# Gate matrix grouped by four expert tiles in DRAM, and a wider spacing of the score tiles

## The chip, the core and the metric

The kernel runs on one core of one Trainium2 chip. Times are device microseconds (us) of the program, from its start to its end. The engines are TensorE (PE; its weight loads are shown apart as PEld), VectorE (DVE), ScalarE (ACT), GpSimd (POOL) and SyncE (SP). SP and ACT issue ordinary DMAs (the queues q1 and q10 of the profile), POOL issues the indirect ones (q0), and all of them run on the same sixteen DMA engines.

## The reference, cut to what matters

A layer has a token mixer and then an expert layer (PEER) over 1024 tokens of width 1024. The change touches the expert layer alone. Each token has 8 heads; each head picks 16 of 16384 experts (128 x 128 product keys), with a softmax over the 16 as gates. Expert e adds gate x gelu(u_e . token) x v_e.

```python
def peer(h, wq, k1, k2, u, v):
    ...
    expert = (jnp.take_along_axis(i1, top_c // PEER_TOPK, axis=-1) * PEER_N_KEYS
              + jnp.take_along_axis(i2, top_c % PEER_TOPK, axis=-1))
    gate = jax.nn.softmax(top_s, axis=-1)
    ...
        act = jax.nn.gelu(jnp.einsum("pd,ped->pe", xb, jnp.take(u, eb, axis=0)), approximate=False)
        return jnp.einsum("pe,ped->pd", (gb * act).astype(v.dtype), jnp.take(v, eb, axis=0))
```

## The kernel before

The 1024 tokens are 8 blocks of 128. Five of them (`DB`: 2, 3, 5, 6, 7, so 640 tokens, `TD`) go the dense way, three (`GB`: 0, 1, 4) the gathered way.

**Dense.** The 16384 experts are 128 tiles of 128. For one tile, `u_load` and `u_turn` bring the rows of `u`, transpose them on PE (`put`, two PSUM buffers) and split them into two f16 halves (`uT`: high half on ACT, low half on POOL by way of `uf`). `u_act` makes the scores of 640 tokens with 48 matmuls (`ph0` and `ph1`, one PSUM buffer each) and applies the gelu on ACT into `ac`, a *score tile*. The scores of 80 of the 128 tiles (`early`, those with `e * 5 % 8 < 5`) are made ahead of time and kept in DRAM (`act_d`, 320 KB each); the other 48 (`live`: 1, 3, 6, 9, ...) are made when they are needed.

**Gates.** `route` finds a block's chosen experts and gates on DVE. `gate_block` builds the dense gate matrix of 32 tokens at a time: for each *chunk* of four tokens DVE writes one-hot rows (`oh`, two instructions), PE multiplies them (`pgm`, 8 matmuls into one PSUM buffer), and ACT copies the result into `gs` (two buffers of 2 MB). After eight chunks the ACT queue stores `gs` into `G_d`. There are 20 such stores and 160 chunks.

**Gathered.** For each of the 128 choices of a token, POOL gathers rows of `u` and of `v` by indirect DMAs (768 in all, 512 KB each, six buffers), and DVE takes a dot product (`row_False`, line 919) or adds into `gacc` (`row_True`, line 924).

**Stages around the change.** `prep` is a generator that runs the routes of blocks 0, 1 and 2, the gating of blocks 2 and 3, the key choice of the second half (`choosing(1)`), and the gating of 5, 6 and 7. It yields a planned cost after each step: 1.65 after a chunk, 16 after a route, 167.6 over the key choice. The loop at its end (lines 1115 to 1122) adds these costs up, and whenever `U_US` (6.2) have come together it places one early score tile (`early_tile`), and with it `G_E` (3.4) gathers once two blocks are routed. Then the expert stage begins, 32 groups of four expert tiles. For a group, the ACT queue loads its gates (`gt4`, two buffers); for each tile the scores are loaded (`acr`) or made, `v_tile` loads and splits the rows of `v`, and `weigh` multiplies scores by gates on DVE and splits them (`w16`: ACT cast, line 1140, and DVE, line 1141). While group g is weighed, `out_unit` multiplies group g - 1 on PE (`pe`, 24 matmuls for each of the five blocks) and DVE adds the result into `acc`. The remaining gathers are spread over the groups by `feed`.

The order of instructions on each engine is set when the program is built, by a scheduler that goes by this program order and the buffers; on the chip each engine runs its list in order. So a wait on ACT also holds the DMAs behind it in the ACT queue.

```python
G_d = dram.tile([TD // NB, P, P, NB], F32, name="G_d")
st_(out=G_d[DB.index(n) * (P // NB) + nb], in_=gs)
st_(out=gt4, in_=G_d[:, :, g * GR:(g + 1) * GR, :].rearrange("b i j n -> i b j n"))
```

In `G_d` a 32-token slice of one second key lies together for all first keys. So a store writes 16 KB for each of the 128 partitions, and a load for four expert tiles reads, for each partition, 20 pieces (one for each 32 tokens) of 4 x 32 x 4 = 512 bytes.

Of the kernel before, what the change touches and what calls it, by code (L numbers as in the profile page):

```python
# [55 lines left out]
R_C, R_CC, R_GM, R_GF, R_AB, R_LB, R_GKB, R_HN, R_GN = 0, 8, 16, 24, 32, 64, 96, 104, 105  # L56


U_US = 6.2
G_E = 3.4  # L60
CS = ((4, 4, 4, 4, 4, 4, 3, 3), (1, 1, 1, 1), 1, 0)
FILL = (0, 0, 2, 0, 0, 1, 1, 0)
# [5 lines left out]
def tile_layer(ctx: ExitStack, tc: tile.TileContext, x, c, ctxt, c_ctx, ada_w, ada_b, norm_mix_g,  # L68
# [51 lines left out]
    yg_d = dram.tile([KC, P, 2, T], F16, name="yg_d")  # L120
    m_d = dram.tile([2 * KC, P, T], F32, name="m_d")
    h2_d = dram.tile([len(GB), P, D], F32, name="h2_d")
    G_d = dram.tile([TD // NB, P, P, NB], F32, name="G_d")
    early = [e for e in range(NKEY) if e * 5 % 8 < 5]
    act_d = dram.tile([len(early), P, TD], F32, name="act_d")

# [823 lines left out]
    def u_load(e):  # L950
        un = pu.tile([P, D], F32, name=f"un{e}", tag="un", bufs=2)
        ld(out=un, in_=u_r[e])
        return un

    def u_turn(e, un):

        uT = pu.tile([P, 2, KC, P], F16, name=f"uT{e}", tag="uT", bufs=2)
        for q in range(2):
            pt = ppu.tile([P, 512], F32, name=f"put{e}_{q}", tag="put", bufs=2)
            for k in range(4):  # L960
                PE.transpose(pt[:, k * P:(k + 1) * P], un[:, (q * 4 + k) * P:(q * 4 + k + 1) * P], ident)  # L961
            pv = pt.rearrange("p (a b) -> p a b", a=4)
            hi, lo = uT[:, 0, q * 4:q * 4 + 4, :], uT[:, 1, q * 4:q * 4 + 4, :]
            S.activation(hi, pv, AF.Copy, scale=SU)  # L964
            uf = pu.tile([P, 4, P], F32, name=f"uf{e}_{q}", tag="uf", bufs=2)
            S.activation(uf, pv, AF.Copy, scale=SU)  # L966
            pace[0] = G.tensor_tensor(out=lo, in0=uf, in1=hi, op=ALU.subtract)  # L967
        return uT
# [15 lines left out]
    with ExitStack() as st:  # L984
# [68 lines left out]
        def gate_block(rT, n, nb):  # L1053

            gs = pg.tile([P, P, NB], F32, name=f"gs{n}_{nb}", tag="gs", bufs=2)
            for t0 in range(0, NB, TB):
                c0 = nb * NB + t0
                oh = pg.tile([P, 4, P, TB], F16, name=f"oh{n}_{c0}", tag="oh", bufs=4)
                cols_ = lambda j: rT[:, j:j + 2, c0:c0 + TB].unsqueeze(2).to_broadcast([P, 2, P, TB])
                tt(V, oh[:, 0:2], iota.unsqueeze(1).to_broadcast([P, 2, P, TB]), cols_(0), ALU.is_equal)  # L1060
                vmark[0] = V.tensor_tensor(out=oh[:, 2:4], in0=oh[:, 1:2].to_broadcast([P, 2, P, TB]), in1=cols_(2), op=ALU.mult)
                pgm = ppg.tile([P, TB, P], F32, name=f"pgm{n}_{c0}", tag="go")
                for t in range(TB):
                    for j in (2, 3):
                        PE.matmul(pgm[:, t, :], lhsT=oh[:, 0, :, t], rhs=oh[:, j, :, t], start=j == 2, stop=j == 3)  # L1065
                S.activation(gs[:, :, t0:t0 + TB].rearrange("p i n -> p n i"), pgm, AF.Copy, scale=SA / SG)  # L1066
                yield 1.65
            st_(out=G_d[DB.index(n) * (P // NB) + nb], in_=gs)

        def gating(blocks, sel):  # L1070
            for bi, n in enumerate(blocks):
# [27 lines left out]
        def early_tile():  # L1099
            nonlocal uT, pend  # L1100
            e = pend
            pend = next(es, None)
            uTn = u_turn(pend, u_load(pend)) if pend is not None else None
            ac = u_act(e, uT)
            st_(out=act_d[early.index(e)], in_=ac)
            uT = uTn
# [7 lines left out]
        for dt in prep():  # L1114
            t_ += dt
            while t_ >= U_US and pend is not None:
                t_ -= U_US
                early_tile()
                if len(gsel) > 1:
                    gathers(G_E)  # L1120
        while pend is not None:
            early_tile()
    prep_st.close()
    if "G" in dbg:
        ld(out=dbg["G"], in_=G_d)
# [9 lines left out]
    def weigh(e, ac, gt4):  # L1135

        v3 = ac.rearrange("p (b n) -> p b n", n=NB)
        tt(V, v3, v3, gt4[:, :, e % GR, :], ALU.mult)
        w16 = pd.tile([P, 2, TD], F16, name=f"w16_{e}", tag="w16", bufs=2 * GR)
        S.copy(w16[:, 0], ac)  # L1140
        vmark[0] = V.tensor_tensor(out=w16[:, 1], in0=ac, in1=w16[:, 0], op=ALU.subtract)
        return w16
# [21 lines left out]
    NU = len(DB)  # L1164
    NG = NKEY // GR
    live = [e for e in range(NKEY) if e not in early]
    uT = u_turn(live[0], u_load(live[0]))
    li = 0
    work = lambda e: 2.1 if e in early else 9.5
    left = [sum(map(work, range(NKEY))), 256 * len(GB) - done[0]]  # L1170

# [4 lines left out]
    for g in range(NG + 1):  # L1176
        cur = None
        if g < NG:
            gt4 = pd.tile([P, TD // NB, GR, NB], F32, name=f"gt{g}", tag="gt4", bufs=2)
            st_(out=gt4, in_=G_d[:, :, g * GR:(g + 1) * GR, :].rearrange("b i j n -> i b j n"))  # L1180
            cur = ([None] * GR, [None] * GR)
            for j in range(GR):
                e = g * GR + j
                if e in early:
                    ac = pu.tile([P, TD], F32, name=f"acr{e}", tag="ac", bufs=3)
                    ld(out=ac, in_=act_d[early.index(e)])
                else:
                    uTn = None
                    if li + 1 < len(live):
                        uTn = u_turn(live[li + 1], u_load(live[li + 1]))  # L1190
                    ac = u_act(e, uT)
                    uT = uTn
                    li += 1
                cur[1][j] = v_tile(e)
                feed(work(e) / 3)
                cur[0][j] = weigh(e, ac, gt4)
                feed(work(e) / 3)
                if prev is not None:
                    for n in DB[j * NU // GR:(j + 1) * NU // GR]:
                        out_unit(g - 1, n, *prev)  # L1200
                feed(work(e) / 3)
        else:
            for _ in gth:
                pass
            m5 = pd.tile([P, D], F32, name="m5", tag="gt4", bufs=2)
            fg = pd.tile([P, D], F32, name="fg", tag="gt4", bufs=2)
            ld(out=m5, in_=mod_d[1:2, :].partition_broadcast(P).rearrange("p a d -> p (a d)"))
            ld(out=fg, in_=final_g.partition_broadcast(P))
            x1s = {}
            for n in range(NT):  # L1210
                x1s[n] = pd.tile([P, D], F32, name=f"x1_{n}", tag="v16", bufs=2 * GR)
                ld(out=x1s[n], in_=x1_d[n * P:(n + 1) * P, :])
                if n in DB:
                    out_unit(g - 1, n, *prev)
                a = acc[n]
                tt(V, a, a, m5, ALU.mult)
                tt(V, a, a, x1s[n], ALU.add)
                ss = pu.tile([P, 2], F32, name=f"fss{n}", tag="fss", bufs=3)
                sq = pu.tile([P, D], F32, name=f"fsq{n}", tag="uT", bufs=2)
                S.activation(sq, a, AF.Square, accum_out=ss[:, 0:1])  # L1220
                S.activation(ss[:, 1:2], ss[:, 0:1], AF.Sqrt, scale=1.0 / D, bias=eps)
                V.reciprocal(out=ss[:, 1:2], in_=ss[:, 1:2])
                V.scalar_tensor_tensor(out=a, in0=a, scalar=ss[:, 1:2], in1=fg, op0=ALU.mult, op1=ALU.mult)
                st_(out=out[n * P:(n + 1) * P, :], in_=a)
        prev = cur
# [27 lines left out]
```

## Time and profile before

| what | us |
|---|---|
| median of 3 runs | 4217.43 (4216.97 to 4219.64) |
| the profiled execution | 4229.67 |
| its span, first to last instruction | 4228.0 |
| PE busy | 3884.8 (92%) |
| DVE busy | 2938.6 (70%) |
| POOL busy | 1683.9 (40%) |
| ACT busy | 1430.1 (34%) |
| DMA traffic | 884.64 MB, 209 GB/s over the span |

A busy share is a mean over stages with different limits: PE is the busiest engine almost everywhere, while DVE and the DMA engines are busy only in the second half, where the expert layer runs. So the stages are read one by one, from tables of stretches; the granted clock is that of PE as a share of full speed, and the DMA share is the mean of the sixteen engines.

### The profile page before, as it was taken

To read this page: it belongs to the slowest core of one execution; us is meant where nothing else is said; L and a number is where in the kernel's file an instruction comes from. 1 tells how busy PE (TensorE), PEld (TensorE's weight loads), DVE (VectorE), ACT (ScalarE), POOL (GpSimd) and SP (SyncE) were. 2 spreads that over 40 slices of the span, in tenths; PEclk is the share of its full clock that TensorE was granted. 3 is DMA by queue.
4 is the path that set the end of the run, shared out by engine and by line. 5 is a ranking of instruction groups with operands and counts; after the bars stand their busy time and mean duration, and the time that the engine had idled before them with its cause. 6 is when DMAs were issued, how large, how long until landed. Compare 5 with 4: busy or idle time off the path is not lost.

```text
span 4228.0 us, 60334 instructions
## 1 busy us (share of the span) xinstructions
PE 3884.8 (92%) x23802; PEld 2350.2 (56%) x23802; DVE 2938.6 (70%) x5132; ACT 1430.1 (34%) x2194; POOL 1683.9 (40%) x1197
## 2 busy tenths in 40 slices
PE   6999999999999999988999989986899989999997
PEld 2665665656655444445776667763445544444453
DVE  5345446242556414379987799977989999889998
ACT  5344444243343202034543334552222222222222
POOL 2011111010011012127655567635766666666663
PEclk9999999999999999999999999987999999999998
DMA  5222122221223583227887778869989999989996
GB/s 189 78 73 85 56 73 79 74 87 46 87 64 115 162 282 107 99 97 242 295 307 249 254 242 298 305 228 319 329 318 336 321 323 325 316 311 325 328 315 232
DMA packets 435306, 884.64 MB, mean 209 GB/s; under 512 B 28511, under 2 KB 245066, under 8 KB 431438
## 3 DMA queue, kind: packets, MB, share of 16 engines
q0 software_dynamic: 110592, 402.70, 27.3%
q1 hardware_dynamic: 202676, 320.19, 22.6%
q10 hardware_dynamic: 121754, 157.89, 10.6%
q8 instruction: 186, 3.05, 0.3%
q14 instruction: 98, 0.80, 0.1%
HBM read 764.80 MB, written 115.88 MB: 208 GB/s over the span
## 4 chain that ended last, share of the span: by engine, by line
PE 47%; DVE 25%; DMA 11%; issue 8%; ACT 6%; POOL 4%; SPq 0%; ACTq 0%; DVEq 0%; POOLq 0%
PE ph L100 5%; DVE row_False L919 5%; PE pe L100 5%; DVE gacc L924 4%; PE pgm L1065 3%; PE pq L100 3%; PE pj_f0h L100 3%; PE pv_g L100 2%; PE pv_h L100 2%; DMA row_False<-in_peer_u_dram,idx 2%; PE pj_f1h L100 2%; PE pj_m L100 2%; DMA vn<-in_peer_v_dram 2%; DMA acr<-act_d 2%; PE pso L100 2%
## 5 line engine op out<-in xcount | busy, mean ns | idle before, releaser
L100 PE MATMUL pe<-v,w 128*128 128x512 f16 x3840 | 883.8, 392 | 138.7 <-DVE acc L1162 104.7
L100 PE MATMUL ph<-hb,uT 128*128 128x256 f16 (+1 forms) x6144 | 892.2, 303 | 14.6 <-POOL uT L967 10.4
L100 PEld LDWEIGHTS <-uT 128*128 128x128 f16 x6144 | 609.4, 99 | 242.5 <-POOL uT L967 13.1
L100 PEld LDWEIGHTS <-w 128*128 128x128 f16 x3840 | 384.0, 100 | 623.0 <-issue 166.4
L940 POOL DMA_INDIRECT row_False<-in_peer_u_dram,idx x384 | 548.9, 1429 | 274.6 <-DVE row_False L919 169.2
L940 POOL DMA_INDIRECT row_True<-in_peer_v_dram,idx x384 | 503.6, 1311 | 264.1 <-DVE gacc L924 173.1
L924 DVE SCALAR_TENSOR_TENSOR gacc<-row_True,dots,gacc 128x1024 f32<-128x1024 f32 x381 | 539.7, 1416 | 39.4 <-DMA row_True<-in_peer_v_dram,idx 35.8
L919 DVE SCALAR_TENSOR_TENSOR row_False<-row_False,h2n 128x1024 f32<-128x1024 f32 x384 | 496.2, 1326 | 67.1 <-DMA row_False<-in_peer_u_dram,idx 66.7
L967 POOL TENSOR_TENSOR uT<-uf,uT 128x512 f16<-128x512 f32 x256 | 380.8, 1499 | 284.0 <-ACT uf L966 282.6
L93 ACT ACTIVATE v<-vn 128x1024 f16<-128x1024 f32 x128 | 135.1, 1055 | 501.9 <-DMA vn<-in_peer_v_dram 386.7
L979 ACT ACTIVATE ac<-ph 128x256 f32<-128x256 f32 (+1 forms) x256 | 110.1, 438 | 371.8 <-PE ph L100 367.1
L1065 PE MATMUL pgm<-oh 128*128 128x128 f16 x1280 | 176.4, 295 | 53.2 <-ACT gs L1066 38.8
L1066 ACT ACTIVATE gs<-pgm 128x512 f32<-128x512 f32 x160 | 171.0, 1069 | 136.6 <-PE pgm L1065 136.6
L94 DVE SCALAR_TENSOR_TENSOR v<-vn,v 128x1024 f16<-128x1024 f32 x128 | 168.2, 1314 | 50.5 <-ACT v L93 50.3
L1162 DVE TENSOR_TENSOR acc<-pe,acc 128x1024 f32<-128x1024 f32 x155 | 188.6, 1217 | 11.8 <-PE pe L100 11.7
L100 PE MATMUL pj_m<-hb,w_m 128*128 128x512 f16 x768 | 187.4, 401 | 2.3 <-DVE lf_g L86 1.6
L1065 PEld LDWEIGHTS <-oh 128*128 128x128 f16 x1280 | 145.7, 117 | 77.0 <-issue 63.5
L100 PE MATMUL pq<-hb,w_wq 128*128 128x512 f16 x768 | 180.0, 387 | 1.0 <-POOL hb L89 0.8
L964 ACT ACTIVATE uT<-put 128x512 f16<-128x512 f32 x256 | 155.0, 605 | 71.0 <-PE put L961 69.4
L89 DVE TENSOR_TENSOR oh<-iota,rTr 128x1024 f16<-128x1024 f16 x160 | 139.1, 879 | 33.9 <-PE pgm L1065 33.8
L100 PEld LDWEIGHTS <-hb 128*128 128x128 f16 x1536 | 150.2, 98 | 17.8 <-issue 0.3
L966 ACT ACTIVATE uf<-put 128x512 f32<-128x512 f32 x256 | 154.4, 603 | 8.9 <-POOL uT L967 8.8
(364 smaller groups left out, 5531.9 us busy)
## 6 DMA issues: line engine op xcount, KB each, us to landing
un<-in_peer_u_dram SPq DMA_DIRECT2D x128, 512.0 KB
vn<-in_peer_v_dram SPq DMA_DIRECT2D x128, 512.0 KB
G_d<-gs ACTq DMA_DIRECT2D x20, 2048.0 KB
gt<-G_d ACTq DMA_DIRECT2D x32, 1280.0 KB
act_d<-ac ACTq DMA_DIRECT2D x80, 320.0 KB
acr<-act_d SPq DMA_DIRECT2D x80, 320.0 KB
mw<-in_ada_w_dram SPq DMA_DIRECT2D x32, 512.0 KB
w_wq<-wq_d SPq DMA_DIRECT2D x32, 512.0 KB
```

Of the source, the lines that this page charges most:

```text
L89: eng.tensor_tensor(out=out, in0=in0, in1=in1, op=op)
L94: return V.scalar_tensor_tensor(out=lo, in0=src, scalar=float(scale), in1=hi, op0=ALU.mult, op1=ALU.subtract)
L100: PE.matmul(ps, lhsT=a(k), rhs=b(k), start=n == 0, stop=n == last)
L919: V.scalar_tensor_tensor(out=row, in0=row, scalar=1.0, in1=h2n, op0=ALU.mult, op1=ALU.mult, accum_out=dots[:, s:s + 1])
L924: V.scalar_tensor_tensor(out=gacc[n], in0=row, scalar=dots[:, s:s + 1], in1=gacc[n], op0=ALU.mult, op1=ALU.add)
L940: G.indirect_dma_start(out=row, out_offset=None, in_=src[0], in_offset=bass.IndirectOffsetOnAxis(ap=gsel[n][0][:, s:s + 1], axis=0))
L964: S.activation(hi, pv, AF.Copy, scale=SU)
L966: S.activation(uf, pv, AF.Copy, scale=SU)
L967: pace[0] = G.tensor_tensor(out=lo, in0=uf, in1=hi, op=ALU.subtract)
L1065: PE.matmul(pgm[:, t, :], lhsT=oh[:, 0, :, t], rhs=oh[:, j, :, t], start=j == 2, stop=j == 3)
L1066: S.activation(gs[:, :, t0:t0 + TB].rearrange("p i n -> p n i"), pgm, AF.Copy, scale=SA / SG)
L1162: vmark[0] = V.tensor_tensor(out=acc[n], in0=ps, in1=acc[n], op=ALU.add)
```

## The change

`G_d` is laid out by groups of four expert tiles: [group, second key, 32-token slice, tile in the group, token]. A load of one group's gates is then one contiguous 10 KB row for each partition; a store of one slice goes out in 32 pieces of 512 bytes for each partition, 4096 in all.

`U_US` goes from 6.2 to 7.2, so early score tiles and their gathers are spaced wider in `prep`. The loop that made the remaining early tiles at the end of `prep` is gone. What is left (`rest`) is put into the first group of the expert stage: a list `todo` orders the tiles that have to be made (two left ones behind each weighing of group 0, the live ones in between), and `next_act` always transposes the tile after the one whose scores it makes. The left tiles are stored into `act_d` like the others and loaded in the last groups.

```diff
-U_US = 6.2
+U_US = 7.2
...
-    G_d = dram.tile([TD // NB, P, P, NB], F32, name="G_d")
+    G_d = dram.tile([NKEY // GR, P, TD // NB, GR, NB], F32, name="G_d")
...
-            st_(out=G_d[DB.index(n) * (P // NB) + nb], in_=gs)
+            st_(out=G_d[:, :, DB.index(n) * (P // NB) + nb].rearrange("g k a n -> k g (a n)"),
+                in_=gs.rearrange("k (g a) n -> k g (a n)", a=GR))
...
-        while pend is not None:
-            early_tile()
...
-    uT = u_turn(live[0], u_load(live[0]))
-    li = 0
+
+    rest = [pend, *es] if pend is not None else []
+    todo = []
+    for j in range(GR):
+        todo += [j] * (j in live) + rest[2 * j:2 * j + 2]
+    todo += rest[2 * GR:] + [e for e in live if e >= GR]
+    if not rest:
+        uT = u_turn(todo[0], u_load(todo[0]))
+    ahead_ = iter(todo[1:])
+
+    def next_act(e):
+        nonlocal uT
+        en = next(ahead_, None)
+        uTn = u_turn(en, u_load(en)) if en is not None else None
+        ac = u_act(e, uT)
+        uT = uTn
+        return ac
+
...
-            st_(out=gt4, in_=G_d[:, :, g * GR:(g + 1) * GR, :].rearrange("b i j n -> i b j n"))
+            st_(out=gt4, in_=G_d[g])
...
-                    uTn = None
-                    if li + 1 < len(live):
-                        uTn = u_turn(live[li + 1], u_load(live[li + 1]))
-                    ac = u_act(e, uT)
-                    uT = uTn
-                    li += 1
+                    ac = next_act(e)
...
+                if g == 0:
+                    for r in rest[2 * j:2 * j + 2] if j < GR - 1 else rest[2 * j:]:
+                        st_(out=act_d[early.index(r)], in_=next_act(r))
```

On ACT, near the end of the gating of block 7 (third of its four stores; `gs` are the copies of the chunks, the other rows belong to tiles), there stands before:

```order
L1066 ACTIVATE gs7_2_24701<-pgm7_68_24718 128x4x128
L964 ACTIVATE uT9_25283<-put9_1_25293 128x512
L966 ACTIVATE uf9_1_25299<-put9_1_25293 128x512
L1066 ACTIVATE gs7_2_24701<-pgm7_72_24731 128x4x128
L1066 ACTIVATE gs7_2_24701<-pgm7_76_24744 128x4x128
L1066 ACTIVATE gs7_2_24701<-pgm7_80_24757 128x4x128
L1066 ACTIVATE gs7_2_24701<-pgm7_84_24770 128x4x128
```

and in the changed program, at the same chunks:

```order
L1066 ACTIVATE gs7_2_23951<-pgm7_68_24052 128x4x128
L966 ACTIVATE uf117_0_24123<-put117_0_24117 128x512
L964 ACTIVATE uT117_24116<-put117_1_24126 128x512
L1066 ACTIVATE gs7_2_23951<-pgm7_72_24065 128x4x128
L966 ACTIVATE uf117_1_24132<-put117_1_24126 128x512
L979 ACTIVATE ac116_24135<-ph0_116_24136 128x256
L1066 ACTIVATE gs7_2_23951<-pgm7_76_24078 128x4x128
L1066 ACTIVATE gs7_2_23951<-pgm7_80_24091 128x4x128
L1066 ACTIVATE gs7_2_23951<-pgm7_84_24104 128x4x128
L979 ACTIVATE ac116_24135<-ph1_116_24162 128x384
L1106 DMA act_d_81<-ac116_24135 128x640
```

Score tiles 116 and 117 now stand between chunks that stood alone; the last of the 75 tiles that are made here is 119.

On ACT at the hand-over (the last gate store, the first gate load `gt0`, the first weighing's cast `w16_0`) there stands before:

```order
L1066 ACTIVATE gs7_3_24807<-pgm7_124_24902 128x4x128
L1068 DMA G_d_80<-gs7_3_24807 128x4096
L1180 DMA gt0_24949<-G_d_80 128x20x128
L93 ACTIVATE v16_0_24955<-vn0_24953 128x1024
L93 ACTIVATE v16_1_25041<-vn1_25039 128x1024
L1180 DMA gt1_25193<-G_d_80 128x20x128
L1140 CAST w16_0_24959<-acr0_24951 128x640
```

and in the changed program:

```order
L1068 DMA G_d_80<-gs7_3_24228 128x32x128
L966 ACTIVATE uf122_1_24551<-put122_1_24545 128x512
L979 ACTIVATE ac120_24554<-ph0_120_24555 128x256
L979 ACTIVATE ac120_24554<-ph1_120_24581 128x384
L964 ACTIVATE uT1_24610<-put1_0_24611 128x512
L1209 DMA act_d_81<-ac120_24554 128x640
L1195 DMA gt0_24520<-G_d_80 128x2560
L93 ACTIVATE v16_0_24526<-vn0_24524 128x1024
L966 ACTIVATE uf1_0_24617<-put1_0_24611 128x512
L964 ACTIVATE uT1_24610<-put1_1_24620 128x512
L966 ACTIVATE uf1_1_24626<-put1_1_24620 128x512
L979 ACTIVATE ac122_24629<-ph0_122_24630 128x256
```

Behind these rows come the second half of the scores of tile 122 and then the first cast, `w16_0`. So the scores of tiles 120 and 122 and the transposes of tile 1 now stand between the last gate store and that cast; tiles 124, 125 and 127 follow behind it, before any output matmul of group 0.

## Rows read from the trace of the kernel before

**Rows 1.** The page's part 2: PE, granted clock and DMA in 40 slices of 105.7 us.

```profile
PE   6999999999999999988999989986899989999997
...
PEclk9999999999999999999999999987999999999998
...
DMA  5222122221223583227887778869989999989996
```

**Rows 2.** Windows: start:end, length, each engine's busy us (instructions), clock, DMA share, GB/s.

```profile
1890.00:1986.90 96.90, 79.11 (x554) 59.29 (x553) 96.54 (x186) 46.00 (x75) 62.50 (x41) 0.91 0.63 205
1986.90:2189.60 202.70, 192.89 (x1458) 152.97 (x1456) 179.02 (x246) 106.13 (x164) 128.11 (x96) 1.00 0.84 302
2189.60:2500.00 310.40, 301.72 (x2028) 204.38 (x2027) 251.25 (x973) 102.58 (x200) 178.49 (x153) 0.99 0.75 257
2500.00:2799.40 299.40, 272.30 (x2029) 215.10 (x2028) 283.26 (x319) 155.28 (x243) 207.24 (x144) 0.97 0.82 295
2799.40:2858.70 59.30, 40.17 (x297) 32.79 (x296) 31.17 (x42) 30.49 (x36) 5.87 (x5) 0.76 0.35 140
2858.70:2876.30 17.60, 0.00 (x0) 0.00 (x0) 1.22 (x1) 2.11 (x2) 0.00 (x0) 0.50 0.84 291
2876.30:2907.80 31.50, 15.99 (x77) 8.11 (x78) 27.57 (x39) 9.48 (x15) 22.26 (x15) 0.72 0.94 321
2907.80:4167.00 1259.20, 1159.08 (x6148) 614.33 (x6149) 1144.82 (x1250) 329.47 (x512) 819.37 (x569) 0.96 0.92 321
```

**Rows 3.** Timeline of the ACT queue in 2650 to 2700: start, length, queue, line, issue.

```profile
2656.80 0.33 ACTq L1068 DMA_DIRECT2D G_d<-gs  x1
...
2681.35 0.33 ACTq L1068 DMA_DIRECT2D G_d<-gs  x1
...
2692.39 0.33 ACTq L1105 DMA_DIRECT2D act_d<-ac  x1
...
2699.78 0.33 ACTq L1105 DMA_DIRECT2D act_d<-ac  x1
```

**Rows 4.** Timeline of 2833 to 2838, PE and ACT: start, length, instruction, idle before.

```profile
2834.08 1.11 PE L1065 MATMUL pgm<-oh 128*128 128x128 f16 x8 [1.14 <-ACT gs L1066]
...
2835.23 1.04 ACT L1066 ACTIVATE gs<-pgm 128x512 f32<-128x512 f32 x1 [1.20 <-PE pgm L1065]
...
2836.33 1.11 PE L1065 MATMUL pgm<-oh 128*128 128x128 f16 x8 [1.13 <-ACT gs L1066]
```

**Rows 5.** Timelines of 2857 to 2909: ACT queue, DVE, PE.

```profile
2858.65 0.33 ACTq L1068 DMA_DIRECT2D G_d<-gs  x1
...
2865.03 0.40 ACTq L1180 DMA_DIRECT2D gt<-G_d  x1
...
2876.32 0.83 DVE L89 TENSOR_TENSOR acr<-acr,gt 128x640 f32<-128x640 f32 x1 [4.62 <-DMA vn<-in_peer_v_dram]
...
2907.76 8.17 PE L100 MATMUL pe<-v,w 128*128 128x512 f16 x28 [1.44 <-DVE w L1141]
```

**Rows 6.** Groups by line, 2500 to 2799.4: busy us, mean ns, idle before.

```profile
L924 DVE SCALAR_TENSOR_TENSOR gacc<-row_True,dots,gacc 128x1024 f32<-128x1024 f32 x86 | 129.4, 1505 | 12.2 <-DMA row_True<-in_peer_v_dram,idx 11.8
```

**Rows 7.** DMA queues, 2859 to 2866: packets, MB, share of 16 engines.

```profile
q10 hardware_dynamic: 144, 2.10, 70.8%
```

**Rows 8.** DMA queues, 1620 to 1650.

```profile
q10 hardware_dynamic: 2176, 1.05, 11.8%
```

**Rows 9.** DMA queues, 2960 to 4100.

```profile
q0 software_dynamic: 62757, 228.51, 56.0%
q1 hardware_dynamic: 31798, 102.24, 24.5%
q10 hardware_dynamic: 72150, 36.71, 11.4%
```

**Rows 10.** Chain of waits, 2907 to 4167: shares by line.

```profile
by line: PE pe L100 14.1%; issue 14.1%; DVE row_False L919 13.0%; DVE gacc L924 10.3%; DMA vn<-in_peer_v_dram 6.5%; DMA acr<-act_d 6.3%; DVE acc L1162 4.8%; DMA row_False<-in_peer_u_dram,idx 4.6%; DVE v L94 4.4%; DVE acr L89 3.8%; DVE w L11
```

**Rows 11.** Groups by line, 2907.8 to 4167.

```profile
L924 DVE SCALAR_TENSOR_TENSOR gacc<-row_True,dots,gacc 128x1024 f32<-128x1024 f32 x242 | 333.4, 1378 | 4.3 <-DMA row_True<-in_peer_v_dram,idx 1.7
```

## The prediction

> **What bounds the kernel now.** I read the slices of the page first [rows 1]: TensorE (PE) is busy in nine tenths or more of nearly every slice, with one dent at about two thirds of the span, where its granted clock falls to 0.7 as well. The DMA engines climb from two or three tenths to nine at the same place. So the next view is a table of stretches, cut at events of the ACT queue [rows 2]. In order they are: the first routes (1890 to 1986.9 us), gating blocks 2 and 3 (A, to 2189.6), the key choice of the second half (B, to 2500), gating 5 to 7 while score tiles last (C, to 2799.4), gating without score tiles (tail, to 2858.7), the wait for the gates (to 2876.3), the first weighing (to 2907.8), and the expert stage (to 4167).
>
> Three things are to be seen. In A and B PE is busy 95% and 97%, so it bounds them; in C PE has 91% and VectorE (DVE) 95%, so both do. From 2799.4 to 2907.8 nothing bounds: PE is busy 56 of 108 us, with the granted clock at 0.5 to 0.76, and DVE is busy 60. In the expert stage PE has 92%, DVE 91% and the DMA engines 92%: three limits within a point.
>
> Why the dent is there: a score tile costs PE 7.4 us where nothing else runs (from one score store to the next), and a block of eight chunks and its tiles lasts some 25 us from gate store to gate store [rows 3]. A gating chunk costs PE 1.1 us, but alone it takes 2.25 us, because PE waits for ACT to empty the one `pgm` buffer and ACT waits for PE [rows 4]. The tail is such chunks one after another, and then comes a chain of DMAs: the last gate block is stored at 2858.65, the first gate load starts 6.4 us later, and the first weighing starts at 2876.32, so 17.7 us in all, with PE idle and the clock at 0.5 (1.2 GHz). The first long run of output matmuls starts at 2907.76 [rows 5].
>
> **The spacing (6.2 to 7.2).** The planner's costs in `prep` sum to 543.6: 160 chunks at 1.65, seven routes at 16, and 167.6 for the key choice. At 6.2 the 80 tiles end after 496, and some 28 chunks are left bare, which is the tail. At 7.2 there is room for 75 tiles, to the last chunk; 5 are left. With each tile go 3.4 gathers, so 5 x 3.4 = 17 gathers move behind the hand-over as well. Stage by stage, with tiles at 7.4 us:
>
> A holds some 2.4 tiles fewer, or 18 us of PE. DVE loses 2.4 x 3.4 gathers at about 1.4 us, and would have 167 of 186 us. I take 16. B holds 167.6/6.2 - 167.6/7.2 = 3.75 tiles fewer, 28 us, with DVE at 81%; I take 26. The first routes give nothing, as DVE is full there (96.5 of 96.9). C with its tail: 206.4 of the costs lie there, so 28.7 tiles instead of 26.1, all between chunks. PE needs 28.7 x 7.4 + 96 x 1.1 = 318 us, and at its 91% of C that is 349. DVE had 283 + 31 and gets 2.6 x 3.4 = 9 more gathers at 1.5 [rows 6], so 328, or 345 at its 95%. Against 358.7 now I take 11 less. Sum: the last gate store comes 53 us sooner.
>
> **The written pieces.** Each of the 20 gate stores goes from 128 pieces of 16 KB to 4096 of 512 bytes. Now one takes 70.8% of 7 us, 4.96 us of the sixteen engines, or 423 GB/s [rows 7]. The nearest row for 512-byte writes is the store of the expert input `h_d`: 11.8% of 30 us for 1.05 MB, 297 GB/s, or 27.7 ns a piece [rows 8]. A store would take 7.1 us then, 2.1 more, 42 us of DMA time in A and C. There the engines have 16 to 18% free, and two `gs` buffers give each store a whole block to land. So I put 4 us on the path; 0 and 42 are the bounds. The last gate store is then at 2858.7 - 53 + 4 = 2809.7.
>
> **The read pieces.** Each of the 32 gate loads goes from 2560 pieces of 512 bytes to 128 of 10 KB. The ACT queue in the expert stage is nearly all gate loads: 11.4% of 1140 us for 36.71 MB, 282 GB/s; beside it the SP queue has 366 and the gathers 358 [rows 9]. At 366 a load takes 3.6 us instead of 4.65, so 34 us less in all; at the 423 of the 16 KB pieces, 50. No row shows a 10 KB piece, and 0 is the lower bound. Against it stand 17 gathers of 0.524 MB at 358 GB/s, 25 us. Net 9 us of 1160 busy. The chain of waits through the expert stage has 17% on three kinds of load (`vn`, `acr`, `row_False`) [rows 10], about 220 us; they shorten by 1 to 2%, so I take 4 us off, and keep 0 and 25. The Trainium skill ("DMA: Bandwidth & Descriptors", Specifications) puts the least transfer for line rate at 512 bytes. By that rule neither side of the new layout costs or gains anything, and the sum below would be 37 again (4 lost, 4 gained, both gone); the rows at 282 and 297 beside 423 GB/s do not bear it out.
>
> **The hand-over.** On ACT the last gate store is now followed by the scores of tile 120, and after the gate load's issue by those of 122, ahead of the cast that needs the gates; on PE six tiles and most of a seventh (122, 1, 124, 125, 127, 3) stand ahead of the first output matmul: 6 x 7.4 + 6 = 50 us of work at full clock, where there were 49 us mostly idle (2858.7 to 2907.8). The gates come after about 18 us as now (2 us more for the store, 1 to 3 less for the load). ACT is blocked by that cast for a few microseconds; `put` has two buffers and `ph` one for each half, so PE has tile 1 to work on meanwhile. Behind the cast on ACT stand score copies and `v` splits, and DVE stands at the weighing from the last chunk on. The loads of that stretch (six `vn`, four `un`, 14 gathers, two gate loads) come to some 15 MB, 47 us at the 321 GB/s of now, so I give output matmuls 56 us after the last store: 2866. PE has then not done about 9 us that it had done by 2907.8 (tile 6 and transposes). Its gain is 2907.8 - 2866 - 9 = 33.
>
> The DVE book gives the same. Its idle time from 1890 to 2907.8 is 148 us now [rows 2]. Afterwards I expect 19 in A, 52 in B, 22 in C, 17 at the wait and 4 later, 114 in all: 34 less. So neither engine arrives at the expert stage with more left than the other, the 17 gathers included, and the stage itself keeps its length but for the 4 us of loads. **Sum: 33 + 4 = 37 us.** From the profiled execution (span 4228.0, 4229.67 with what lies around it) that gives 4192.7; it lies 12.2 above the median, so on the median 4217.4 - 37 = 4180.
>
> **Rivals.** (1) *The 17 gathers are paid in full.* In the expert stage DVE, PE and DMA lie within a point of each other, so work that arrives late has no cover: 17 x 1.38 us on DVE = 23 [rows 11], and the loads gain nothing. 33 - 23 = 10, so 4207. For it: DVE's 91%. Against it: the idle book, in which DVE catches up before the stage.
> (2) *A to C do not shorten.* If DVE bounds them already, half of the 53 us goes, 27, and what is left of the hand-over is about 6: 4211. For it: DVE at 95% in C. Against: B, where it has 81%.
> (3) *Slower: the written pieces.* Consecutive pieces of one partition lie 1.25 MiB apart, which no row shows. A and C have 125 us of DMA time free, the stores take 99 now, and 224 us over 81920 pieces on 16 engines is 44 ns a piece. From there every nanosecond costs 5.1 us and gathers, `gs` and the tail all wait. At 51 ns the gain is gone; at 60, twice the row of `h_d`, 82 - 37 = 45 us are lost: 4262.
> (4) *The loads matter more.* With the engines at 92%, 50 us less of gate pieces and the better mix may take 25 us off the chain's loads rather than 4: 4159.
> That the change does not do what it says is excluded for the order: the rows of the built program show the tiles spread to the last chunk and five behind it.
>
> **How the numbers follow.** Forecast (4166 to 4196) 0.55; (4) 0.12; (1) 0.14; (2) 0.10; (3) 0.09. A measurement of this kernel tells about 0.2%, 8.4 us, from no change. Faster than 4209: the forecast, (4), 0.08 of (1) and 0.03 of (2), so 0.78. Within 0.2%: 0.05 of (1) and 0.05 of (2), 0.10. Slower: (3), and 0.01 and 0.02 of (1) and (2), 0.12. The range 4148 to 4212 holds the forecast, nearly all of (4) and (1) and half of (2), and leaves (3) and the rest out.
>
> **What would show it.** The dent in PE's slices is gone, and the granted clock stays above 0.9 there. The last gate store comes at 2800 to 2820, the first weighing 16 to 20 us later, the long output matmuls at 2855 to 2880. A gate store's share gives 25 to 31 ns a piece, and the ACT queue in the expert stage 350 GB/s or more. The expert stage from there lasts 1255 to 1265 us less what PE has in hand. Wrong would be: blocks in C still 25 us apart (2), a gate store over 40 ns a piece (3), or an expert stage longer by 20 us and more with DVE at 93% (1).

## The result, and the profile after

The changed kernel is slower: 4248.52 us, median of 5 runs (4239.62 to 4254.23), ratio to the kernel before 1.0067, 95% interval 1.0046 to 1.0088. The forecast was 4180; the measured time lies above the whole range (4148 to 4212). The profiled execution took 4249.52 us (span 4247.5); before it was 4229.67 (4228.0).

The page's part 2 (PE, granted clock, DMA in 40 slices) of the changed kernel answers to [rows 1]:

```profile
PE   6999999999999999988899988888899989989997
...
PEclk9999999999999999999999999999999999999998
...
DMA  5222122221214573227887778889888999888987
```

The dent at two thirds of the span is gone, and so is the fall of the clock. But PE's row has new eights ahead of that place, where there were nines (slices 20, 25 and 26). The windows of the changed kernel (start:end, length, then busy us and instructions of PE, PEld, DVE, ACT and POOL, clock, DMA share, GB/s) are cut at gate stores: A runs from the first to the eighth (first row), B to the ninth (second row), C to the last (third row).

```profile
1972.70:2172.20 199.50, 179.33 (x1314) 139.65 (x1313) 168.99 (x255) 100.40 (x149) 104.19 (x80) 0.97 0.84 273
2172.20:2495.80 323.60, 306.71 (x2076) 211.04 (x2075) 274.97 (x1017) 115.77 (x217) 193.57 (x156) 0.98 0.74 251
2495.80:2814.50 318.70, 281.35 (x2098) 223.21 (x2097) 273.39 (x305) 161.12 (x243) 188.76 (x134) 0.96 0.84 278
2814.50:2835.00 20.50, 12.77 (x91) 9.10 (x89) 1.17 (x2) 4.53 (x9) 1.79 (x2) 0.90 0.91 309
2907.80:3225.00 317.20, 287.80 (x1504) 151.65 (x1502) 274.06 (x359) 79.24 (x124) 207.95 (x141) 0.95 0.86 308
```

[rows 2] cut B and C at 2500, which is 52 us ahead of the ninth gate store of the kernel before. Cut at that store, as above, its B and C are:

```profile
2189.60:2552.00 362.40, 344.10 (x2320) 235.87 (x2319) 303.25 (x1036) 128.46 (x242) 218.95 (x179) 0.98 0.75 256
2552.00:2858.65 306.65, 270.10 (x2034) 216.40 (x2031) 262.43 (x297) 159.89 (x237) 172.65 (x123) 0.94 0.75 273
```

B, within which no gate store is issued, is 39 us shorter. A holds fewer tiles, yet it is hardly shorter, 199.5 us instead of 202.7: PE has 90% of it instead of 95%, DVE 85% instead of 88%. C is 12 us longer, with PE at 88% and DVE at 86%, the shares that it had with the bare chunks in it. So in the stretches with gate stores something new takes time. What took it is on ACT. The timeline of ACT and its queue in the changed kernel around a gate store in C (start, length, instruction, idle before), which answers to [rows 3]:

```profile
2617.61 0.38 ACTq L1068 DMA_DIRECT2D G_d<-gs  x1
...
2623.87 0.49 ACT L979 ACTIVATE ac<-ph 128x384 f32<-128x384 f32 x1 [3.52 <-PE ph L100]
2624.31 0.60 ACT L964 ACTIVATE uT<-put 128x512 f16<-128x512 f32 x1
2624.39 10.62 ACTq L1106 DMA_DIRECT2D act_d<-ac  x1
2635.07 0.60 ACT L966 ACTIVATE uf<-put 128x512 f32<-128x512 f32 x1 [10.16 <-issue]
```

The gate store itself is issued in 0.38 us. The next DMA of the ACT queue, a score store, then takes **10.62 us to issue**, where [rows 3] has 0.33 for the same instruction, and ACT does nothing meanwhile. The DMA queues in these stretches (packets, MB, share of 16 engines), first 2624.4 to 2635, then 2635 to 2637:

```profile
q10 hardware_dynamic: 3116, 1.59, 49.9%
...
q10 hardware_dynamic: 747, 0.57, 84.0%
```

The queue is working off pieces of the gate store all that time, three quarters of its 4096. In the program the score store waits for one semaphore, that of the gelu on ACT, which was done at 2624.36. So it is the issue itself that is held until most of the store's pieces have gone; some 680 of the 4096 are left when it ends. This happens after 13 of the 20 gate stores, for over 1 us each; the 80 score stores take 90.3 us to issue instead of 26.2, 64 us more of ACT. What ACT copies late (`gs`, `uf`) PE gets late, and `pgm` has one buffer. The group of the `gs` copies, 1890 to 2880 (busy, mean ns, idle before and what ended it), first of the kernel before, then of the changed one:

```profile
L1066 ACT ACTIVATE gs<-pgm 128x512 f32<-128x512 f32 x160 | 171.0, 1069 | 136.6 <-PE pgm L1065 136.6
```

```profile
L1066 ACT ACTIVATE gs<-pgm 128x512 f32<-128x512 f32 x160 | 170.9, 1068 | 179.2 <-PE pgm L1065 138.2 <-issue 39.1 <-DMA act_d<-ac 1.3
```

The 39.1 us that end with "issue" are new. Then the hand-over and the reads: the ACT queue and DVE of the changed kernel, answering to [rows 5], and the DMA queues of 2960 to 4100, answering to [rows 9].

```profile
2814.47 0.38 ACTq L1068 DMA_DIRECT2D G_d<-gs  x1
2819.77 2.15 ACTq L1209 DMA_DIRECT2D act_d<-ac  x1
2825.88 0.35 ACTq L1195 DMA_DIRECT2D gt<-G_d  x1
...
2834.97 1.78 DVE L89 TENSOR_TENSOR acr<-acr,gt 128x640 f32<-128x640 f32 x1
```

```profile
q0 software_dynamic: 62528, 227.65, 56.3%
q1 hardware_dynamic: 30922, 99.44, 24.3%
q10 hardware_dynamic: 3888, 35.39, 7.9%
```

The last gate store is 44 us sooner, the first weighing 41. The gate loads run at 35.39 MB in 7.9% of 1140 us, 393 GB/s instead of 282. And still the last `acc` comes 20 us later (4234.44 instead of 4214.92), so some 61 us were lost between the first weighing and the end.

### The profile page after: what moved, and what is told of

It reads as the page before. It is cut to its first block, busy times and chain, and to the rows that moved or that the text cites. A ratio compares the mean times of both kernels' runs of the same rounds, so it can differ in the third digit from the quotient of the medians.

```text
span 4247.5 us, 60389 instructions
## 1 busy us (share of the span) xinstructions
PE 3890.3 (92%) x23802; PEld 2353.6 (55%) x23802; DVE 2935.3 (69%) x5132; ACT 1427.4 (34%) x2194; POOL 1682.9 (40%) x1197
## 3 DMA queue, kind: packets, MB, share of 16 engines
q1 hardware_dynamic: 202676, 320.19, 22.7%
## 4 chain that ended last, share of the span: by engine, by line
PE 51%; DVE 20%; DMA 11%; issue 8%; ACT 5%; POOL 3%; ACTq 1%; SPq 0%; DVEq 0%; POOLq 0%
PE ph L100 7%; PE pe L100 6%; DVE row_False L919 4%; PE pq L100 3%; DVE gacc L924 3%; DMA row_False<-in_peer_u_dram,idx 3%; PE pgm L1065 3%; PE pj_f0h L100 3%; PE pv_g L100 2%; PE pv_h L100 2%; DMA row_True<-in_peer_v_dram,idx 2%; PE pj_f1h L100 2%; PE pj_m L100 2%; PE pso L100 2%; PE pj_qh L100 2%
## 5 line engine op out<-in xcount | busy, mean ns | idle before, releaser
L100 PE MATMUL ph<-hb,uT 128*128 128x256 f16 (+1 forms) x6144 | 901.4, 304 | 15.8 <-POOL uT L967 14.8
L940 POOL DMA_INDIRECT row_False<-in_peer_u_dram,idx x384 | 526.5, 1371 | 271.3 <-DVE row_False L919 173.8
L940 POOL DMA_INDIRECT row_True<-in_peer_v_dram,idx x384 | 514.3, 1339 | 251.5 <-DVE gacc L924 160.3
L919 DVE SCALAR_TENSOR_TENSOR row_False<-row_False,h2n 128x1024 f32<-128x1024 f32 x384 | 515.7, 1375 | 105.7 <-DMA row_False<-in_peer_u_dram,idx 105.3
L924 DVE SCALAR_TENSOR_TENSOR gacc<-row_True,dots,gacc 128x1024 f32<-128x1024 f32 x381 | 524.4, 1376 | 21.3 <-DMA row_True<-in_peer_v_dram,idx 18.6
L967 POOL TENSOR_TENSOR uT<-uf,uT 128x512 f16<-128x512 f32 x256 | 390.5, 1539 | 332.3 <-ACT uf L966 331.1
L89 DVE TENSOR_TENSOR oh<-iota,rTr 128x1024 f16<-128x1024 f16 x160 | 126.9, 811 | 56.7 <-PE pgm L1065 56.7
```

The lines of the kernel that those rows point to most:

```text
L100: PE.matmul(ps, lhsT=a(k), rhs=b(k), start=n == 0, stop=n == last)
L919: V.scalar_tensor_tensor(out=row, in0=row, scalar=1.0, in1=h2n, op0=ALU.mult, op1=ALU.mult, accum_out=dots[:, s:s + 1])
L924: V.scalar_tensor_tensor(out=gacc[n], in0=row, scalar=dots[:, s:s + 1], in1=gacc[n], op0=ALU.mult, op1=ALU.add)
L940: G.indirect_dma_start(out=row, out_offset=None, in_=src[0], in_offset=bass.IndirectOffsetOnAxis(ap=gsel[n][0][:, s:s + 1], axis=0))
```

## The experiments

Theory P held that work moved behind the hand-over (17 gathers, 5 tiles) is paid in the expert stage; its first rival L, that the layout itself costs. The first four kernels took the change apart. The windows of time of these four were written for a kernel before of 4217 us; beside them it took 4225.66, so they are read here by the ratios.

**e1, the layout alone.** The order of all engines is that of the kernel before.

```diff
-U_US = 7.2
+U_US = 6.2
```

> Only the new layout of the gate matrix; the spacing is 6.2 again, so the order of all engines is that of the kernel before. Theory P (work that was moved behind the hand-over, 17 gathers and 5 score tiles, is paid in the expert stage): 4205 to 4222, no change or a little faster, since the gate loads move at about 390 GB/s instead of 282. Rival L (the layout costs: the last gate store takes 11.4 us instead of 6.4 to its load, and 10 KB pieces disturb the gathers): 4232 to 4248, slower than before by 15 to 30, with the expert stage longer.

Measured 4256.25, ratio 1.0068 (1.0054 to 1.0081): the layout alone costs as much as the whole change. By the ratio that is 4246, in the window of L. L holds, but not as it was put: the timelines of 2136 to 2160, before and in e1, show the same two instructions of ACT's queue:

```profile
2137.36 0.33 ACTq L1068 DMA_DIRECT2D G_d<-gs  x1
...
2141.43 0.33 ACTq L1105 DMA_DIRECT2D act_d<-ac  x1
```

```profile
2140.24 0.38 ACTq L1068 DMA_DIRECT2D G_d<-gs  x1
...
2144.32 8.44 ACTq L1106 DMA_DIRECT2D act_d<-ac  x1
...
2145.18 0.33 SPq L952 DMA_DIRECT2D un<-in_peer_u_dram  x1
...
2152.80 1.02 ACT L1066 ACTIVATE gs<-pgm 128x512 f32<-128x512 f32 x1 [7.39 <-issue]
```

The delay grows where gate stores are: the gate store is 15 us late at the end of A, 15 at the start of C and 27 at its end (2886.03 instead of 2858.65). From there little is added and nothing won: the first gate load is 29.7 late, that of group 20 28.3, the last `acc` 31.8. So the 10 KB reads, faster as they are, bring nothing to this stage. The score stores take 78.2 us to issue. While ACT is held, SP issues a load in 0.33 us (third row). In the four kernels with 4096 pieces whose score stores stay on ACT, SP issued 44 loads while an issue on ACT was held for over 1 us, each in 0.33 us. So it is the ACT queue that is held, not both. The Trainium skill ("Perfetto Trace Analysis", DMA Instruction — HWDGE (DVE, Sync)) says that a sequencer locks a descriptor generator, shared by the two that issue such DMAs, after its semaphores are satisfied, and that this time is in the profile. That the time is in the profile, and comes after the semaphores, agrees with the 8.44 us. That it is a lock on the shared generator does not fit SP's rows; what it is instead, no run here tells.

**e2, the spacing and the left tiles alone** (`rest` in group 0, 17 gathers owed), with the old layout of `G_d`, its store and its load.

> Only the spacing of 7.2 with the five left tiles in group 0; the gate matrix has its old layout (16 KB written, 512 bytes read). Theory P (moved work is paid): 4238 to 4256, like the changed kernel. Rival L (layout): 4180 to 4205, with the hand-over's gates after 18 us and DVE's waits for gathered rows in groups 4 to 10 back at 6 us.

Measured 4228.27, ratio 1.0006 (0.9997 to 1.0016): no change, and between the windows of L and of P (by the ratio 4220). No issue on ACT lasts over 0.42 us, and the last gate store comes at 2791.63, 67 us sooner than in the kernel before and 22.8 sooner than in the changed one. So the change is two things: a layout that costs 28 us, and a spacing that brings 67 us at the last gate store and nothing at the end.

**e3, the 17 gathers back into `prep`** (`G_E = 3.64`), and **e4, the five left tiles at the end of `prep`** (the old loop kept), each in the changed kernel.

> The changed kernel with 3.64 gathers per score tile in prep instead of 3.4, so that about 17 more of them are done before the hand-over, as many as in the kernel before; score tiles as in the changed kernel. Theory P, gathers: the stage gets its 17 x 1.38 = 23 us back and prep gives 0 to 10 of it away: 4224 to 4236. Rival H (the left tiles at the hand-over put POOL behind and the gathers starve in groups 4 to 10, whatever their number): 4240 to 4252, with DVE's waits for gathered rows still at 35 us in groups 4 to 10.

> The changed kernel, but the five left tiles are made at the end of prep, ahead of the expert stage, as the kernel before would have done. Theory P, gathers: the 17 gathers are still late, so 4240 to 4255. Rival H (left tiles between the first weighings): the waits for gathered rows in groups 4 to 10 fall back to 6 us, and the time is 4215 to 4232. If the five tiles are paid for wherever they stand after the last gating chunk: 4240 to 4260.

Measured 4241.37, ratio 1.0037 (1.0023 to 1.0051), and 4241.2, 1.0035 (1.0021 to 1.0048). Each takes about half of the loss back. By the ratios e3 is 4233, in P's window, and e4 4232, below P's and at the edge of that of H. Rival H is that the left tiles, put between the first weighings, starve the gathers. But H had told of DVE's waits for gathered rows as well: these are 35.6 us in 2907.8 to 3225 of the changed kernel, 16.5 in e3, where H left them at 35, and 26.7 in e4, where H took them to 6. With the held ACT in both, they could not say more.

**e5 and e9, the held issue.** e5 is the changed kernel with the score stores of `prep` on SP's queue, so that hardly anything stands behind a gate store on ACT. e9 has the order of the kernel before and a layout by eight tiles: 2048 pieces of 1 KB written, 512-byte pieces read.

```diff
-            st_(out=act_d[early.index(e)], in_=ac)
+            ld(out=act_d[early.index(e)], in_=ac)
```

> The changed kernel (new layout, spacing 7.2), but the score stores of prep are issued from the SP queue instead of the ACT queue, so that nothing stands behind a gate store on ACT for the length of a block. Theory Q (the issue of the next store waits until the 4096 pieces of the gate store have been taken, and this holds the ACT engine, 64 us in the changed kernel): the long issues leave ACT, the last gate store comes near 2792 as with the old layout, and the time is 4215 to 4234. Rival W (the 512-byte writes themselves take the DMA engines' time from the gathers and tile loads): 4240 to 4256, with the last gate store still at 2810 or later.

```diff
-    G_d = dram.tile([NKEY // GR, P, TD // NB, GR, NB], F32, name="G_d")
+    G_d = dram.tile([NKEY // 8, P, TD // NB, 8, NB], F32, name="G_d")
```

> The order of the kernel before (spacing 6.2) with a layout grouped by eight expert tiles: a gate store goes out in 2048 pieces of 1 KB instead of 4096 of 512 bytes, a gate load reads 2560 pieces of 512 bytes as in the kernel before. Theory Q (the issue behind a gate store is held while its pieces are waiting, so the number of pieces counts): the long issues on ACT fall from 50 us to 15 or less and the time to 4218 to 4234. Rival W (only the bytes and the writes' share of the DMA engines count, which is the same): 4240 to 4258, as with 512 bytes.

e9: 4223.54, ratio 0.9999 (0.9989 to 1.0010). With half the pieces the cost is gone. Rival W, the DMA engines' time for the writes, is not the same here, as its window took it: by the packets' times, in the mean of the 20, a gate store takes the sixteen engines 5.3 us before, 6.4 in e9 and 7.5 in e1. So by W half of e1's 28 us should be left, and none is. Of the idle time that ended with "issue" on ACT, 1890 to 2850, one row is left:

```profile
ACT uf L966 <- issue: 1.8, 1, 1.8
```

e5: 4243.69, ratio 1.0039 (1.0025 to 1.0053), above the window of Q and inside that of W, while the last gate store, at 2806.07, lies between Q's 2792 and W's 2810. A lasts 191.2 us (190.0 in e2, 199.6 in the changed kernel), C to the last gate store 309.1 (305.6 and 318.7): 18 of the 22.7 us come back there. But the key choice B, which has no gate store, is 9 us longer than in e2, and the rest is lost in the stage. So what e5 shows is the stretches. Its total takes 12 of the 28 us back; that the rest is what the moved stores do to SP's loads is not shown.

**e6, e7, e13: what is owed.** All with the old layout and spacing 7.2: e6 is e2 with 3.64 gathers a tile, e7 is e2 with the left tiles at the end of `prep`, e13 both.

> Old layout, spacing 7.2 with five left tiles in group 0, and 3.64 gathers a tile, so that as many gathers are done before the hand-over as in the kernel before. Theory P (17 gathers behind the hand-over cost their 23 us of DVE in full, since DVE has no free time in the expert stage): 4204 to 4218, 10 to 23 less than with 3.4. Rival S (the stage takes back any lead): 4222 to 4232, the same as with 3.4.

> Old layout, spacing 7.2, 3.4 gathers a tile, the five left tiles at the end of prep, ahead of the first group: the spacing of the change alone. Theory H (the left tiles between the first weighings put uT on POOL and with it the gathers behind): 4212 to 4222, and DVE's waits for gathered rows in groups 4 to 10 fall from 37 us. Rival S: 4224 to 4234.

> The kernel before with spacing 7.2 and 3.64 gathers a tile: the five left tiles stand at the end of prep, and no gathers are owed. If the two things that are owed make the loss between 2908 and 3225 together: DVE's waits for gathered rows there fall from 33 to 6 to 10 us and the time is 4196 to 4207, as with spacing 6.78. If the spacing itself does it: 4208 to 4218 with waits of 18 us and more.

Measured: e6 4209.95, ratio 0.9962 (0.9949 to 0.9976); e7 4217.19, 0.9988 (0.9974 to 1.0002); e13 4202.1, 0.9950 (0.9936 to 0.9964). Against e2's 1.0006 that is 19, 8 and 24 us, of which the 8 are hardly clear of the noise. The first ten groups of the stage show a part of it. Waits (total us, times, longest) in 2907.8 to 3225 of e2, then of e13; the kernel before has 6.2 us there:

```profile
DVE row_False L919 <- DMA row_False<-in_peer_u_dram,idx: 32.8, 9, 7.1
```

```profile
DVE row_False L919 <- DMA row_False<-in_peer_u_dram,idx: 13.0, 6, 6.2
```

The 13.0 lie between e13's two windows for these waits; its time lies in the one for what is owed.

**e8, e15, e14, e16: the spacing.** The kernel before with `U_US` 6.78 (80 tiles just fit), 6.6, and 6.95 with `G_E` 3.5 (two tiles left, made at the end of `prep`, no gathers owed); e16 is the last with the two tiles in group 0, as the change does it.

> The kernel before with a spacing of 6.78 and nothing else: the planned costs of prep sum to 543.6, so all 80 tiles and their 272 gathers just fit to the last chunk, none is left over and no gathers move behind the hand-over. Theory P (work moved behind is what eats the gain): the bare tail of 59 us goes, nothing is owed: 4190 to 4210, faster than before by 0.3 to 0.7%. Rival S (a lead at the hand-over is lost in the stage whatever is owed): 4218 to 4230.

> The kernel before with spacing 6.6: all 80 tiles and 272 gathers before the last chunk, nothing owed, and some 9 bare chunks, about 20 us of them instead of 59. Where the bare chunks are what 6.78 gains: 4202 to 4212, between 6.2 (4221) and 6.78 (4201).

> The kernel before with spacing 6.95 and 3.5 gathers a tile: two tiles left, at the end of prep, no gathers owed. If what is owed costs: 4196 to 4208, near the spacing of 6.78. If the spacing itself costs: half way to that of 7.2, 4204 to 4214.

> Old layout, spacing 6.95, 3.5 gathers a tile, and the two left tiles in group 0 as in the change: no gathers owed, and the two tiles fill PE while the gates come. If left tiles at the hand-over are free where no gathers are owed: 4190 to 4203, the fastest. If they hold the gathers behind uT: 4204 to 4214, above the same spacing with them at the end of prep.

Measured: e8 4201.46, ratio 0.9940 (0.9926 to 0.9954); e15 4217.54, 0.9985 (0.9977 to 0.9994); **e14 4185.93, 0.9913 (0.9899 to 0.9927)**, the fastest of all, 36 us under the kernel before; e16 4191.75, 0.9924 (0.9908 to 0.9941). e8 lies in P's window, and e16 in the one for left tiles that are free. e15 lies above its window, so the bare chunks are not all that 6.78 gains, and e14 lies below both of its own. Two left tiles in group 0 cost nothing that these intervals tell.

**e10, e11, e12: more gathers in `prep`.** Spacing 6.78 with 3.8 and 4.2 gathers a tile, and e2 with 4.0.

> The kernel before with spacing 6.78 and 3.8 gathers a tile: 32 more gathers are made in prep. Theory P (DVE bounds the expert stage, and still has some 130 us idle in prep between 2000 and 2850): each gather taken out of the stage saves its 1.38 us and costs less than that in prep; 4176 to 4196. Rival F (prep is full at 3.4 gathers: more of them lengthen the blocks by what they save): 4198 to 4208, as with 3.4.

> As before with spacing 6.78, and 4.2 gathers a tile: 64 more gathers in prep, 88 us of DVE. Theory P: 4160 to 4190, if the DVE takes them in its idle time of prep; where blocks and key choice get longer by more than half of it, 4185 to 4200. Rival F: 4200 to 4225.

> Old layout, the change's spacing of 7.2 and its left tiles in group 0, with 4.0 gathers a tile: about 45 more of them in prep than at 3.4. Theory P: 17 of them bring 18 us (as at 3.64), the other 28 up to 1.38 us each: 4175 to 4200. Rival H (the left tiles between the first weighings cost the start of the stage, however many gathers are owed): 4202 to 4215, above what 6.78 gives.

Measured 4226.11, 4223.54 and 4220.4, ratios 1.0004, 1.0005 and 0.9992, each with 1 in its interval. The last gate store moves from 2826.67 (e8) to 2861.76 and 2891.9, so the gathers do lengthen the blocks. That is F; e11 lies in F's window, e10 above it. e12 lies above both of its windows; its last gate store is at 2836.38, 45 us behind that of e2.

**A book at one time.** To compare the kernels I counted what each had finished at 2907.8 and at 3225 us (gathers used, `acc`, weighings, `v` splits; output units and score tiles on PE), and priced the difference to the kernel before: on DVE 1.38 us a gather, 1.22 an `acc`, 1.65 a weighing, 1.32 a split, on PE 5.54 an output unit (24 matmuls) and 7.4 a tile, parts of a unit counted as parts. Plus is ahead. The last column compares the profiled executions; the one before was 12 us above its median.

| kernel | DVE at 2907.8 | DVE at 3225 | PE at 3225 | span against before |
|---|---|---|---|---|
| changed | -1 | -21 | -1 | +19.5 |
| e1 layout | -25 | -25 | -27 | +31.7 |
| e2 spacing, left tiles | +18 | +1 | +15 | -4.2 |
| e7 | +19 | +5 | +18 | -12.8 |
| e6 | +34 | +18 | +13 | -19.8 |
| e13 | +32 | +24 | +20 | -27.0 |
| e8 | +23 | +27 | +25 | -26.0 |
| e14 | +35 | +29 | +25 | -39.4 |
| e16 | +32 | +30 | +26 | -39.1 |
| e10 | +33 | +24 | -5 | -3.9 |
| e11 | +54 | +34 | -30 | 0.0 |
| e12 | +38 | +11 | -16 | +5.3 |

In these and the other kernels of this study the end moves about as the lesser of the two leads at 3225 does, within 15 us; e11 is the exception, better than PE's lag. So more gathers bring nothing: they buy DVE's lead with PE's. The lead of DVE that is lost in these ten groups is 17 us where gathers and five tiles are owed (e2; 20 in the changed kernel), 14 and 17 where one of them is (e7, e6), 8 and 7 where only tiles at the end of `prep` are (e13, e14), 2 with two tiles in group 0 (e16) and none in e8. But e11 and e12, which owe no gathers, lose 20 and 27, so what is owed is not the only thing that eats a lead.

## Why the prediction was wrong, point by point

**The dent, the clock, the last gate store**: as forecast, the last gate store at 2814.47 (2800 to 2820). But that is two errors that cancel in part: the spacing brought 67 us (e2) where 53 were forecast, and the pieces took 22.8 where 4 were. Of the 67, 14 came before the first gate store (1986.92, in e2 1972.84), where the forecast put nothing because DVE is full; then 13 in A (16 forecast) and 40 in B and C together (37).

**The written pieces: the term that failed first.** Their price was right. In 2814.4 to 2826.5 the ACT queue has 67.9% of 12.1 us, 8.2 us, of which 1.1 is other traffic (0.43 MB): 7.1 us a store, 28 ns a piece, against 27.7 forecast and 44 in rival (3). So (3) named the place and the sign, but not the mechanism. What failed is the sentence that two `gs` buffers give each store a whole block to land. I looked at who waits for the buffer, and not at what is queued behind the store on its engine: the score store, and with its issue all of ACT. No row of before showed an issue that is held: there the stores went out in 128 pieces, and no score store took over 0.36 us to issue. The bound of 42 us on the path did hold it (22.8 at the last gate store, 29 to 32 in e1). The rule of the Trainium skill ("DMA: Bandwidth & Descriptors", Specifications) that 512 bytes are enough for line rate, which the prediction weighed, is not borne out: 512-byte pieces were written at 295 GB/s and read at 282, 16 KB pieces written at 423 and 10 KB pieces read at 393.

**The read pieces**: the rate was forecast at 350 GB/s or more and is 393, and the gain at 4 us, where e1 shows none.

**The hand-over and "the stage keeps its length": the second failure.** The first weighing came 20.5 us after the last gate store (16 to 20 forecast). The long output matmuls were to come 56 us after it, at 2855 to 2880; they came 74 us after it, in e2 73. PE of the changed kernel, answering to the last row of [rows 5]:

```profile
2888.67 10.23 PE L100 MATMUL pe<-v,w 128*128 128x512 f16 x38 [6.91 <-ACT w L1139]
```

DVE was to be 34 us ahead and PE 33. With the old layout e2 was 18 and 27 ahead at 2907.8, so half of the gain was there on DVE and four fifths on PE: the hand-over took 17 us more than forecast, about what the first routes had brought beyond the forecast (14). Then DVE lost 17 us in ten groups, and 20 in the changed kernel, where it had no lead to lose. The forecast had DVE catch up in its idle time and dismissed rival (1) by that. (1) was near the price: with the gathers made in `prep`, e6 gets 19 us back where (1) had 23. But its sign, DVE at 93% in the stage, did not come: DVE has 90% from 2907.8 to 4185 in the changed kernel. It waits for gathered rows instead, in 2907.8 to 3225, first before, then in the changed kernel:

```profile
DVE row_False L919 <- DMA row_False<-in_peer_u_dram,idx: 6.2, 2, 5.9
```

```profile
DVE row_False L919 <- DMA row_False<-in_peer_u_dram,idx: 35.6, 10, 6.7
```

e6, e7 and e13 show that what is owed costs 24 us of e2's time, most of it the gathers; by the book DVE of e13 is 14 us further ahead at 2907.8 and loses 9 less behind it. How the owed work costs this is only argued. The chain of waits of the changed kernel, 2890 to 3235, in order of time (start, us, what; the longest pieces):

```profile
2969.48 1.15 DVE acc L1161
2970.67 12.21 PE pe L100 x48
...
2986.72 1.19 POOL uT L967
...
2991.16 2.19 issue
2993.35 1.57 POOL row_False L940
2995.22 9.49 DMA row_False<-in_peer_u_dram,idx
...
3005.97 1.15 DVE acc L1161
```

DVE frees the PSUM of an output unit, PE runs two units and then turns the next tile, POOL can only then split `uT` and issue the gather that stands behind it, and DVE waits for that gather's rows. With fewer gathers done at the same group, this loop would close more often. What stays open is the 8 us that e13 loses there and the 20 and 27 of e11 and e12, what takes the 74 us at the hand-over, and why 6.95 beats 6.78 by 0.3% at the same lead.

**The sum**: -37 was forecast; measured is +28 (0.67% of 4217). About 28 of the difference are the layout's (e1, and the changed kernel beside e2), and the other 37 are the gain of the spacing, which e2 shows as nothing at the end. That the layout costs by the held issues is shown by e9 and, in the stretches with gate stores, by e5; over e5's whole time only 12 of the 28 came back.

## What to carry to other kernels

A DMA that is cut into more pieces is not only dearer on the DMA engines: ask what is issued next on the same queue, and by which engine, because that engine may stand still until most of the pieces are gone. A lead at a hand-over is worth what the worse of the two busy engines keeps of it some hundred us later; count what each has done at one time, and count what was moved behind the hand-over as part of the price. Here the better edit was the plain one: the layout left alone, no gathers owed, and a spacing that just fits (0.9940) or leaves two tiles (0.9913).

## What the runs showed of the hardware that was not expected

The issue of a DMA behind one of 4096 pieces of 512 bytes on the same queue took up to 11.12 us (e4; 10.62 in the changed kernel), with its semaphore satisfied, while SP issued on its own queue in 0.33 us. Behind a DMA of 2048 pieces the longest such issue was 2.8 us, and only three of 80 were over 1 us. It is not a matter of writes or of the new layout: behind the old gate load of 2560 pieces, a score store took 2.3 to 3.8 us to issue in e7, e13 and e14, where left tiles stand at the end of `prep`. The ACT queue of e14:

```profile
2821.63 0.40 ACTq L1180 DMA_DIRECT2D gt<-G_d  x1
...
2822.60 3.77 ACTq L1105 DMA_DIRECT2D act_d<-ac  x1
```

Behind a store of 128 pieces of 16 KB one issue of 1.46 us was seen, in e8, 0.9 us after the store; the other runs with such stores show none over 0.42 us.
